# Moving all elementwise work from GpSimd to VectorE in a hybrid S5 + latent-attention layer, with a three-operation recurrence

## The chip, the cores and the metric

One core of a Trainium2 chip runs the whole program. The metric is device time in microseconds. Before the change the median of 3 runs is 2492.51 us (2489.13 to 2495.65).

## What is computed

One layer is applied to a prompt (512 tokens) and to a sample group (8 sequences of 8 tokens over a paged cache of 1024 positions), with the same weights. Cut to what matters here:

```
proj = x @ w_in                    # split: u (1024) | cq (512) | ckv (512) | kr (64)
bu   = einsum('bsgh,gph->bsgp', u, b_bar)          # S5: 64 groups, 64 complex states
h    = associative_scan(a_bar, bu)                 # h[t] = a_bar*h[t-1] + bu[t]
y    = real(einsum('bsgp,ghp->bsgh', h, c)) + d*u ; g = gelu(y)
out  = g * sigmoid(g @ w_glu + b_glu)
q    = (rms_norm(cq) @ w_uq) ; ckv = rms_norm(ckv) ; krope = rope(kr)
o    = softmax(q_lat.ckv + q_rope.krope) @ ckv     # prompt causal, sample over pages
x    = layer_norm(alpha*x + concat(out, o@w_uv) @ w_out)
x    = layer_norm(alpha*x + (silu(x@w_gate) * (x@w_up)) @ w_down)
```

All is float32. A product of two float32 matrices is made of three matmuls on rounded parts (`hi` by ScalarE, `lo = value - hi`).

## The kernel before, in words

The 576 token columns are held in two halves of 288. Stages follow each other in time: the input product (17 blocks of 128 output columns, each 96 matmuls 128x288) with S5's parameters, chunk sums, recurrence and taps beside it (0 to about 305 us of the profile); queries and prompt attention with S5's output (to about 500); sample attention, gate and output product with the first layer norm (to about 960); the feed-forward part (to the end), whose last 200 us hold the sums of w_down and the second layer norm.

A planner (`Clock`) records every instruction at build time: it keeps an estimated end time for each engine and tile, and generator fibers (`merge`, `drive`) are resumed when their data is estimated to be ready, so PE's order is written out by these estimates. A scheduler then orders each engine's queue by priority. All instructions are issued through one helper line, so every row of the profile says L180 and is told apart by the names of its tiles. Each engine runs its queue in order; SP's queue issues most DMAs.

Where the change acts:

- `sooner` chose between VectorE (DVE) and GpSimd (POOL) for an elementwise instruction, by the planner's estimates. It serves `split` (the `lo` parts: tiles `wlo`, `xl`, `cktlo`, `cknlo`), `rope`, and the sums and layer norms of the output and feed-forward stages (tiles `z`, `g`, `m`, `xl`, `Ah`, `Al`, `QS`, `T`, which are buffers used again under old names).
- `s5_states` makes for each of 8 chunks of 8 channel groups the factor `G` (four products, two sums, a transpose to `Gt`) and then PE's sums `Gt * U` into `S`. Two products (`Gx`, `Gy`) were on POOL. `U` is the chunk of u, written to DRAM (`us`) and read back in another order.
- `s5_scan` runs 63 steps over blocks of 8 tokens. Tile `S` was stored state first, block last (so one block's 64 numbers lie 72 apart), with five DVE instructions a step. At its end `S` went to DRAM (`Sd`) in four DMAs; `s5_out` reads it as `H2` (tile `H` in the rows).
- `s5_taps` makes for each chunk `P` (from `pw` and `bc`) and `BB`, all on POOL, and PE multiplies them (tile `ks`).
- `weights` builds the ring of later weights; its first two are of w_kv, used right after the queries of heads 0 and 1.

Of the kernel before, what the change touches and what calls it, by code (L numbers as in the profile page):

```python
# [7 lines left out]
F32 = mybir.dt.float32  # L8
# [154 lines left out]
class Clock:  # L163
# [356 lines left out]
class Layer:  # L520
# [248 lines left out]

    def place(self, j):  # L770

        j -= 16
        if j < 2:
            return None
        if j == 2:
            hi, lo = self.ff.tile([128, 1024], F32R, name="E"), self.cst.tile([128, 1024], F32R, name="rp")
            return [[x[:, 256 * i:256 * i + 256] for x in (hi, lo)] for i in range(4)]
        if j == 3:
            return [list(x) for x in zip(self.t4[:4], self.t4[4:])]
        a, b = (('T2', 'B22'), ('B11', 'B21'))[j // 2 - 2]  # L780
        k = j % 2 * 2
        return self.X[a][k:k + 2] + self.X[b][k:k + 2]

# [187 lines left out]
    def s5_side(self, done, lat):  # L971
        yield from self.s5_params(done)
        yield lambda: done['u']
        self.s5a = lat.enter_context(self.pool("s5a"))

        def states():
            with self.pool("s5b") as self.s5b:
                yield from self.s5_states(done)
            done['s5'] = True
            yield from self.s5_scan()  # L980
# [75 lines left out]
    def s5_params(self, done):  # L1056
# [5 lines left out]
        with self.pool("s5t") as tp:  # L1062
# [113 lines left out]
            nc.vector.tensor_copy(self.a8, V[:, 8])  # L1176

            Q = new((128, 10, 2, 128))
            for g2 in range(2):
                p = self.mmp(bufs=4)  # L1180
                for pb in range(2):
                    for i, e in enumerate((1, 2, 4, 9)):
                        nc.tensor.matmul(p[:, pb, 64 * i:64 * i + 64], sel[:, 2 * g2 + pb],
                                         V[:, e].rearrange("p r k -> p (r k)"), start=True, stop=True)
                yield
                for i in range(4):
                    nc.scalar.activation(Q[:, i].rearrange("p r (k a b) -> p b r k a", a=2, b=2)[:, :, :, :, g2],
                                         p[:, :, 64 * i:64 * i + 64].rearrange("p b (r k) -> p b r k", r=2), AF.Copy)
                yield
# [44 lines left out]

    def s5_states(self, done):
# [3 lines left out]
        pt = nc.gpsimd.tensor_tensor  # L1239
        self.S = self.s5a.tile([128, 32, 2, NC], F32, name="S")  # L1240
        self.h0s = self.s5a.tile([128, 32, 2, 8], F32, name="h0s")
        nc.sync.dma_start(self.h0s, io['h0s'].rearrange("p (a b c) -> p a b c", a=32, b=2))

        def load(ck):
            bq = p.tile([128, 2, 16, 16], F32, name="bq", bufs=2)
            nc.sync.dma_start(bq, io['s5bq'][ck].rearrange("p (r a b) -> p r a b", r=2, a=16))
            return bq

        bq = load(0)
        prev = None  # L1250
        for ck in range(9):
            cur = None
            if ck < 8:
                yield lambda: done['u'] > ck
                yield self.when(self.us[ck])
                U = self.load_U(p, ck)
                nb = load(ck + 1) if ck < 7 else None
# [9 lines left out]
                yield self.when(x, y)  # L1267
# [4 lines left out]
                cur = (U, Gt, ck)  # L1272
                bq = nb
            if prev:
                U, Gt, pk = prev
                yield self.when(U, Gt)
                ps = self.mmp(bufs=4)
                for g in range(8):
                    for r in range(2):
                        o = (g // 2 % 2) * 2 * NC + r * NC  # L1280
                        nc.tensor.matmul(ps[64 * (g % 2):64 * (g % 2) + 64, g // 4, o:o + NC],
                                         Gt[:, r, g], U[:, g], start=True, stop=True)
                yield
                nc.scalar.activation(self.S[:, 4 * pk:4 * pk + 4].rearrange("p (a k) r c -> p a (k r c)", a=2),
                                     ps[:, :, :HALF], AF.Copy)
            prev = cur

    def s5_scan(self):
        nc, io, S = self.nc, self.io, self.S
        tt, pt = nc.vector.tensor_tensor, nc.gpsimd.tensor_tensor  # L1290
        w = self.s5a.tile([128, 32, 2, 8], F32, name="scw")
        b8 = lambda r: self.a8[:, r, :, None].to_broadcast([128, 32, 8])
        h = self.h0s
        for (r, ra, op) in ((0, 0, OP.add), (0, 1, OP.subtract), (1, 0, OP.add), (1, 1, OP.add)):
            tt(w[:, :, r], h[:, :, r if ra == 0 else 1 - r], b8(ra), OP.mult)
            tt(S[:, :, r, PC:], S[:, :, r, PC:], w[:, :, r], op)
        so2 = self.s5a.tile([128, 32, 2, 8], F32, name="scw")
        nc.vector.tensor_copy(so2, S[:, :, :, PC:])
        nc.sync.dma_start(io['o_ss'].rearrange("p (k r b) -> p k r b", r=2, b=8), so2)
        yield self.lag('DVE')  # L1300
        ab = self.a8[:, 0, :, None].to_broadcast([128, 32, 2])
        t1 = self.s5a.tile([128, 32, 2], F32, name="sc1")
        t2 = self.s5a.tile([128, 32, 2], F32, name="sc2")
        nai = self.s5a.tile([128, 32], F32, name="nai")
        nc.vector.tensor_scalar(nai, self.a8[:, 1], -1.0, None, op0=OP.mult)
# [8 lines left out]
        nc.gpsimd.tensor_copy(so, S[:, :, :, PC - 1])  # L1314
        yield self.when(so)
        nc.sync.dma_start(io['o_sp'].rearrange("p (k r) -> p k r", r=2), so)
        for r in range(2):
            for g2 in range(2):
                nc.sync.dma_start(self.Sd[64 * r:64 * r + 64, g2::2, 1:PC], S[64 * g2:64 * g2 + 64, :, r, :PC - 1])

    def s5_taps(self):

        nc, io, pool = self.nc, self.io, self.s5k
        pt = nc.gpsimd.tensor_tensor
# [10 lines left out]
        def powers():  # L1335
            for ck in range(8):
# [14 lines left out]
                X = X.rearrange("p a b c -> p (a b c)")[:, :128].rearrange("p (g h) -> p g h", g=8)  # L1351
                pt(BB[:, :, :16], bc[:, 0], fb(0), OP.mult)
                pt(X, bc[:, 1], fb(1), OP.mult)
                pt(BB[:, :, :16], BB[:, :, :16], X, OP.add)
                for s in (slice(4), slice(4, 8)):
# [4 lines left out]
                    yield self.lag('POOL')  # L1360
# [1095 lines left out]
```

## Time and profile before

| | |
|---|---|
| median of 3 runs | 2492.51 us |
| profiled execution | 2493.54 us, of which the span is 2491.5 |
| PE busy | 2350.2 us (94%) |
| DVE busy | 1957.2 us (79%) |
| ACT busy | 1077.4 us (43%) |
| POOL busy | 444.4 us (18%) |

The span is the time from the first to the last instruction that the profiler recorded; 2 us lie around it. A busy PE can be slow: the column PEclk gives the share of the full TensorE clock that was granted. PE is the engine with the most work; where it idles, the row behind the idle time names the instruction that released it. POOL works up to about 950 us and after 2300 us; between 960 and 2000 us it has nothing to do.

### The profile page before, as it was taken

The numbers are of one execution on the slowest core, as the hardware profiler recorded it, in microseconds if no ns is written. First come the engines' busy times: TensorE is split into PE (matmuls) and PEld (weight loads), VectorE is DVE, ScalarE is ACT, GpSimd is POOL, SyncE is SP. The second block draws the span as 40 slices with busy tenths as digits, with TensorE's granted clock in tenths as the row PEclk, the third lists the DMA queues.
The fourth block names the chain that finished last, engine by engine and source line by source line (L and its number), as shares of the span: only waits on it lengthen the run. The fifth ranks groups of instructions, "written<-read, shape, count | busy, mean of one in ns | idle before, by whom it ended". The sixth has DMA issues, their size and how long they took to land.

```text
span 2491.5 us, 45005 instructions
## 1 busy us (share of the span) xinstructions
PE 2350.2 (94%) x17220; PEld 2297.1 (92%) x17220; DVE 1957.2 (79%) x3313; ACT 1077.4 (43%) x1685; POOL 444.4 (18%) x390
## 2 busy tenths in 40 slices
PE   8988989999899989999999999999999999979995
PEld 7877989998898989999999999999999999979994
DVE  7759766778778886999988878887778876755978
ACT  4221355656555544433333333333336644553133
POOL 2682010143344550000000000000000000000335
PEclk9988999999999989999999999999999999989997
DMA  6563456478765556455433333333236765677622
GB/s 216 178 183 120 105 161 199 144 240 294 243 194 165 198 172 217 174 183 190 164 113 132 120 113 132 112 123 107 107 113 208 254 186 143 170 205 251 243 94 76
DMA packets 219161, 419.90 MB, mean 169 GB/s; under 512 B 62210, under 2 KB 127106, under 8 KB 217154
## 3 DMA queue, kind: packets, MB, share of 16 engines
q1 hardware_dynamic: 187154, 359.66, 43.5%
q10 hardware_dynamic: 30064, 44.98, 5.0%
q0 software_dynamic: 1728, 12.39, 2.8%
q8 instruction: 135, 2.21, 0.4%
q14 instruction: 80, 0.66, 0.1%
HBM read 337.52 MB, written 83.64 MB: 169 GB/s over the span
## 4 chain that ended last, share of the span: by engine, by line
PE 56%; DVE 12%; DMA 11%; issue 3%; ACT 3%; POOL 1%; SPq 0%; ACTq 0%; DVEq 0%; POOLq 0%
PE mm L180 34%; PE sc L180 21%; DVE wlo L180 3%; DVE z L180 2%; DVE xl L180 2%; DMA wraw<-w_gu 2%; DMA hraw<-hd 1%; PE po L180 1%; DMA cktraw<-ckt 1%; DMA mraw<-so 1%; DVE T L180 1%; ACT whi L180 1%; DMA T<-pa 1%; DVE Al L180 1%; DVE g L180 1%
## 5 line engine op out<-in xcount | busy, mean ns | idle before, releaser
L180 PE MATMUL mm<-xh,whi 128*128 128x288 f32 x2272 | 606.1, 305 | 17.5 <-ACT xh L180 9.6
L180 PE MATMUL mm<-xh,wlo 128*128 128x288 f32 x2272 | 607.1, 304 | 13.6 <-DVE wlo L180 13.3
L180 PE MATMUL mm<-xl,whi 128*128 128x288 f32 x2272 | 605.7, 303 | 4.5 <-DVE xl L180 4.0
L180 PEld LDWEIGHTS mm<-xh,whi 128*128 128x128 f32 x2272 | 409.8, 193 | 26.8 <-ACT xh L180 10.9
L180 PEld LDWEIGHTS mm<-xh,wlo 128*128 128x128 f32 x2272 | 410.6, 193 | 20.9 <-DVE wlo L180 18.0
L180 PEld LDWEIGHTS mm<-xl,whi 128*128 128x128 f32 x2272 | 411.1, 193 | 7.8 <-DVE xl L180 5.0
L180 PE MATMUL sc<-z,whi 128*128 128x288 f32 x1470 | 350.8, 297 | 1.2 <-ACT z L180 0.6
L180 ACT ACTIVATE whi<-wraw 128x1024 fp32r<-128x1024 f32 (+2 forms) x159 | 173.8, 1094 | 281.1 <-PE mm L180 187.2
L180 DVE TENSOR_TENSOR wlo<-wraw,whi 128x1024 fp32r<-128x1024 f32 (+2 forms) x150 | 214.4, 1431 | 89.7 <-ACT whi L180 87.4
L180 ACT ACTIVATE whi<-E 128x1024 fp32r<-128x1024 f32 x120 | 127.2, 1060 | 334.7 <-issue 193.1
L180 PEld LDWEIGHTS sc<-z,whi 128*128 128x128 f32 x1470 | 250.7, 189 | 2.3 <-ACT whi L180 1.0
L180 ACT ACTIVATE whi<-rp 128x1024 fp32r<-128x1024 f32 x120 | 127.4, 1061 | 256.9 <-issue 191.3
L180 DVE TENSOR_TENSOR wlo<-E,whi 128x1024 fp32r<-128x1024 f32 x120 | 146.7, 1223 | 94.0 <-ACT whi L180 93.5
L180 POOL DMA_DIRECT2D pa<-m x6 | 5.3, 890 | 1200.2 <-ACT m L180 1200.2
L180 PE MATMUL mm<-T,H 128*128 128x288 f32 x1200 | 217.3, 296 | 1.8 <-ACT T L180 1.7
L180 DVE TENSOR_TENSOR wlo<-rp,whi 128x1024 fp32r<-128x1024 f32 x120 | 146.5, 1221 | 72.1 <-ACT whi L180 71.9
L180 PEld LDWEIGHTS mm<-T,H 128*128 128x128 f32 x1200 | 180.8, 189 | 2.5 <-ACT T L180 2.2
L180 PE MATMUL mm<-Ah,wlo 128*128 128x288 f32 x480 | 137.5, 308 | 14.6 <-DVE wlo L180 12.7
L180 PE MATMUL sc<-Ah,H 128*128 128x288 f32 x552 | 144.3, 297 | 6.6 <-DVE H L180 3.2
L180 PE MATMUL mm<-Ah,H 128*128 128x288 f32 x552 | 144.4, 297 | 4.2 <-ACT Ah L180 4.2
L180 PE MATMUL sc<-z,wlo 128*128 128x288 f32 x490 | 145.8, 298 | 0.9 <-DVE wlo L180 0.9
L180 PE MATMUL sc<-g,whi 128*128 128x288 f32 x490 | 144.8, 295 | 0.9 <-ACT g L180 0.8
(505 smaller groups left out, 5493.6 us busy)
## 6 DMA issues: line engine op xcount, KB each, us to landing
wraw<-w_gu SPq DMA_DIRECT2D x145, 512.0 KB, 3.2
qns<-w_gu SPq DMA_DIRECT2D x59, 512.0 KB, 3.3
wraw<-w_out SPq DMA_DIRECT2D x56, 512.0 KB, 3.9
wraw<-w_dq SPq DMA_DIRECT2D x43, 512.0 KB, 3.4
cktraw<-ckt SPq DMA_DIRECT2D x64, 320.0 KB, 4.5
cknraw<-ckn SPq DMA_DIRECT2D x64, 256.0 KB, 3.9
hd<-QS ACTq DMA_DIRECT2D x16, 1008.0 KB, 4.1
wraw<-w_in SPq DMA_DIRECT2D x14, 1024.0 KB, 5.8
```

The lines of the kernel that those rows point to most:

```text
L180: r = f(*a, **k)
```

## The change

Six edits: `sooner` always returns VectorE; the products of `s5_states` and `s5_taps` that were on GpSimd go to VectorE; `S` is stored block first, so that one recurrence step is one product of 128 numbers and two sums of 64; `G` is made by a fiber of its own, up to one chunk ahead of PE's sums, and `B`'s first load and the state `h0` stand earlier; `S` is copied by ScalarE into a staging tile (`hst`, two buffers, four pieces of eight state groups) and goes to `Sd` in 16 DMAs; the first two weights of the later ring are split at an earlier priority. GpSimd keeps memsets, small casts and the DMAs that add.

```diff
     def sooner(self, op, out, *ins):
-        t = self.ready(*ins)
-        d, p = (max(t + 150, self.end[e]) + self.cost(e, op, out, ins) for e in ('DVE', 'POOL'))
-        return self.gpsimd if p + 500 < d else self.vector
+        return self.vector
...
         self.ring = Ring(self, self.wst, "w", 1024, items, ahead=100)
+        at = self.tc.cur_priority
+        self.tc.cur_priority = max(at - 400, 0)
+        self.ring.split(1)
+        self.tc.cur_priority = at
...
-        yield from self.merge((states(), 3), (taps(), 1))
+        yield from self.merge((states(), 1e9), (taps(), 1))
...
-        self.S = self.s5a.tile([128, 32, 2, NC], F32, name="S")
+        self.S = self.s5a.tile([128, NC, 2, 32], F32, name="S")
...
-                pt(x, B[1], E[1], OP.mult)
-                pt(y, B[1], E[0], OP.mult)
+                yield self.when(bq)
                 tt(G[:, 0], B[0], E[0], OP.mult)
+                tt(x, B[1], E[1], OP.mult)
                 tt(G[:, 1], B[0], E[1], OP.mult)
+                tt(y, B[1], E[0], OP.mult)
...
+                yield ('t', nc.ready(U, made[ck]) + 4000)
                 ps = self.mmp(bufs=4)
...
+                for a in range(2):
+                    k = 4 * ck + 2 * a
+                    nc.scalar.activation(self.S[:, :, :, k:k + 2].rearrange("p c r k -> p k r c"),
+                                         ps[:, a, :HALF].rearrange("p (k r c) -> p k r c", k=2, r=2), AF.Copy)
...
         for c in range(1, PC):
-            tt(t1, S[:, :, :, c - 1], ab, OP.mult)
-            tt(t2[:, :, 0], S[:, :, 1, c - 1], nai, OP.mult)
-            tt(t2[:, :, 1], S[:, :, 0, c - 1], self.a8[:, 1], OP.mult)
-            tt(S[:, :, :, c], S[:, :, :, c], t1, OP.add)
-            tt(S[:, :, :, c], S[:, :, :, c], t2, OP.add)
-            yield self.lag('DVE', 2000)
+            tt(x, S[:, c - 1, :, None, :].to_broadcast([128, 2, 2, 32]), A, OP.mult)
+            tt(S[:, c], S[:, c], x[:, 0], OP.add)
+            tt(S[:, c], S[:, c], x[:, 1], OP.add)
+            yield self.lag('DVE', 1500)
...
-        for r in range(2):
-            for g2 in range(2):
-                nc.sync.dma_start(self.Sd[64 * r:64 * r + 64, g2::2, 1:PC], S[64 * g2:64 * g2 + 64, :, r, :PC - 1])
+        n = 32 // 4
+        for k in range(0, 32, n):
+            yield ('t', hp.avail("hst", 2))
+            st = hp.tile([128, n, 2, PC - 1], F32, name="hst", bufs=2)
+            nc.scalar.activation(st, S[:, :PC - 1, :, k:k + n].rearrange("p c r k -> p k r c"), AF.Copy)
+            yield self.when(st)
+            for r in range(2):
+                for g2 in range(2):
+                    nc.sync.dma_start(self.Sd[64 * r:64 * r + 64, 2 * k + g2:2 * (k + n):2, 1:PC],
+                                      st[64 * g2:64 * g2 + 64, :, r])
...
-        pt = nc.gpsimd.tensor_tensor
+        pt = nc.vector.tensor_tensor
...
-                    yield self.lag('POOL')
+                    yield self.lag('DVE', 2500)
```

VectorE's queue where the first two chunks of S5 are worked on. Before (`wlo` is the low part of a w_in block, waited for by that block's matmuls):

```order
L180 TENSOR_TENSOR wlo<-wraw,whi 128x2048
L180 TENSOR_SCALAR nai<-a_276 128x32
L180 TENSOR_TENSOR scw<-h0s,a_276 128x32x8 x2
L180 TENSOR_TENSOR G<-bq,eq 128x512 x2
L180 TENSOR_TENSOR G<-G,Gx 128x512
L180 TENSOR_TENSOR G<-G,Gy 128x512
L180 STREAM_TRANSPOSE Gt<-G 128x1024
L180 TENSOR_TENSOR G<-bq,eq 128x512 x2
```

The same place of the changed kernel:

```order
L180 TENSOR_TENSOR P<-bc,pw 128x576
L180 TENSOR_TENSOR G<-G,Gx 128x512
L180 TENSOR_TENSOR P<-bc,pw 128x576
L180 TENSOR_TENSOR PX<-bc,cf 128x128
L180 TENSOR_TENSOR BB<-bc,cf 128x8x16
L180 TENSOR_TENSOR G<-G,Gy 128x512
L180 TENSOR_TENSOR wlo<-wraw,whi 128x2048
L180 TENSOR_TENSOR Gx<-bq,eq 128x512
```

The products of the taps (`P`, `PX`, `BB`) and `Gx`, `Gy` now stand between VectorE's own, and a `wlo` stands behind a `P` that waits for the DMAs of `pw` and `bc`.

SP's queue at the end of the recurrence, before:

```order
L180 DMA Sd<-S 2048x1x63 x3
L180 DMA o_sp<-so 128x64
L180 DMA Sd<-S 2048x1x63
L180 DMA wraw<-w_kv 128x1024 x2
L180 DMA U<-us_60 128x576
```

And in the changed kernel:

```order
L180 DMA Sd<-hst 64x8x63 x2
L180 DMA o_sp<-so 128x64
L180 DMA Sd<-hst 64x8x63 x13
L180 DMA wraw<-w_kv 128x1024 x2
L180 DMA Sd<-hst 64x8x63
L180 DMA U<-us_60 128x576
```

The loads of w_kv stand behind 15 of the 16 pieces of the state, the last of which come from the fourth staging copy.

## Rows read from the trace of the kernel before

**Rows 1.** Busy time by stage: each line is a stretch (us), its length, then busy us (and instruction count) of PE, PEld, DVE, ACT and POOL, then the granted share of TensorE's clock, the DMA share and GB/s.

```profile
0.00:320.00 320.00, 276.37 (x2179) 267.57 (x2180) 241.39 (x578) 98.29 (x133) 137.54 (x145) 0.93 0.53 161
320.00:500.00 180.00, 176.16 (x1262) 166.97 (x1261) 126.69 (x301) 108.67 (x226) 13.81 (x36) 0.98 0.54 165
500.00:960.00 460.00, 426.10 (x2908) 405.88 (x2906) 372.85 (x540) 252.97 (x395) 201.35 (x143) 0.94 0.66 216
960.00:2000.00 1040.00, 1033.63 (x7739) 1028.95 (x7739) 864.05 (x1358) 420.36 (x595) 0.00 (x0) 1.00 0.43 150
2000.00:2300.00 300.00, 282.55 (x2021) 275.86 (x2020) 188.63 (x295) 144.29 (x237) 11.12 (x13) 0.96 0.66 185
2300.00:2491.50 191.50, 155.36 (x1121) 151.92 (x1120) 163.64 (x245) 52.83 (x102) 80.63 (x55) 0.92 0.40 144
```

**Rows 2.** PE in order of time: start, length, what, and in brackets PE's idle time before it and what ended it.

```profile
39.67 0.85 PE L180 MATMUL mm<-xl,whi 128*128 128x288 f32 x2 [4.02 <-DVE xl L180]
...
127.50 0.66 PE L180 MATMUL mm<-P,BB 128*32 128x128 f32 x8 [5.12 <-POOL P L180]
143.91 0.43 PE L180 MATMUL mm<-P,BB 128*32 128x128 f32 x8 [2.33 <-POOL P L180]
...
210.40 0.85 PE L180 MATMUL mm<-xh,wlo 128*128 128x288 f32 x2 [5.93 <-DVE wlo L180]
239.63 0.64 PE L180 MATMUL mm<-ones,rssq 128*96 128x1 f32 x3 [5.19 <-DVE rssq L180]
318.08 0.38 PE L180 MATMUL mm<-whi,xh 128*128 128x256 f32 x1 [4.66 <-ACT whi L180]
639.86 0.80 PE L180 MATMUL po<-cknlo,PT 128*128 128x512 f32 x1 [3.45 <-DVE cknlo L180]
904.94 0.40 PE L180 MATMUL mm<-Ah,wlo 128*128 128x288 f32 x1 [2.73 <-DVE wlo L180]
920.06 0.61 PE L180 MATMUL mm<-Ah,wlo 128*128 128x288 f32 x1 [6.93 <-DVE wlo L180]
2453.08 0.40 PE L180 MATMUL mm<-g,Ah 128*128 128x288 f32 x1 [2.91 <-DVE Al L180]
```

**Rows 3.** DVE and POOL in order of time, in three places; columns as in rows 2.

```profile
15.24 7.97 DVE L180 SCALAR_TENSOR_TENSOR sp<-sp,sp 128x32 f32<-128x32 f32 x6
28.37 0.52 DVE L180 SCALAR_TENSOR_TENSOR sp<-sp,sp 128x32 f32<-128x32 f32 x4
15.16 1.32 POOL L180 TENSOR_TENSOR wlo<-wraw,whi 128x512 fp32r<-128x512 f32 x1 [13.98 <-ACT whi L180]
16.44 1.43 POOL L180 TENSOR_TENSOR xl<-xr,xh 128x576 fp32r<-128x576 f32 x1
...
917.58 2.42 DVE L180 TENSOR_TENSOR wlo<-wraw,whi 128x1024 fp32r<-128x1024 f32 x1
923.47 1.21 DVE L180 TENSOR_TENSOR wlo<-wraw,whi 128x1024 fp32r<-128x1024 f32 x1
...
2475.08 5.65 POOL L180 TENSOR_TENSOR Al<-Al,xh 128x576 f32<-128x576 f32 x3
2479.39 1.95 DVE L180 TENSOR_TENSOR z<-z,xh 128x576 f32<-128x576 f32 x1
2481.93 0.74 DVE L180 TENSOR_TENSOR z<-z,xh 128x576 f32<-128x576 f32 x1
```

**Rows 4.** Groups of DVE and ACT instructions by shape up to 350 us: busy us, mean ns of one, idle time before them.

```profile
L180 DVE TENSOR_TENSOR G<-bq,eq 128x512 f32<-128x512 f32 x16 | 19.7, 1269 | 0.2
L180 DVE TENSOR_TENSOR G<-G,Gy 128x512 f32<-128x512 f32 x8 | 10.9, 1368 | 1.0 <-POOL Gy L180 1.0
L180 DVE TENSOR_TENSOR wlo<-wraw,whi 128x512 fp32r<-128x512 f32 x9 | 6.1, 688 | 6.0 <-ACT whi L180 6.0
L180 DVE TENSOR_TENSOR sp<-sp 128x128 f32<-128x128 f32 x7 | 1.8, 286 | 0.1
L180 ACT ACTIVATE whi<-wraw 128x1024 fp32r<-128x1024 f32 x5 | 5.2, 1054 | 2.5 <-DMA wraw<-w_uq 2.5
```

**Rows 5.** Groups of POOL instructions by shape up to 350 us, in the same columns.

```profile
L180 POOL TENSOR_TENSOR P<-P,PX 128x576 f32<-128x576 f32 x16 | 29.8, 1862 | 0.9
L180 POOL TENSOR_TENSOR PX<-bc,pw 128x576 f32<-128x576 f32 x16 | 21.0, 1314 | 0.7
L180 POOL TENSOR_TENSOR P<-bc,pw 128x576 f32<-128x576 f32 x16 | 20.0, 1270 | 23.2 <-DMA pw<-pwd 23.2
L180 POOL TENSOR_TENSOR PX<-bc,cf 128x128 f32<-128x128 f32 x8 | 4.6, 569 | 8.8 <-DMA bc<-s5bc 8.8
```

**Rows 6.** DVE in one step of the recurrence that POOL does not disturb; columns as in rows 2.

```profile
212.36 0.59 DVE L180 TENSOR_TENSOR S<-S,sc 128x64 f32<-128x64 f32 x2
212.98 0.27 DVE L180 TENSOR_TENSOR sc<-S,a 128x64 f32<-128x64 f32 x1
213.17 0.20 DVE L180 TENSOR_TENSOR sc<-S,nai 128x32 f32<-128x32 f32 x1
213.28 0.19 DVE L180 TENSOR_TENSOR sc<-S,a 128x32 f32<-128x32 f32 x1
213.40 0.58 DVE L180 TENSOR_TENSOR S<-S,sc 128x64 f32<-128x64 f32 x2
```

More of the change, by code (lines that the diff above doesn't have):

```diff
@@ L979, in states @@
             done['s5'] = True
-            yield from self.s5_scan()
+            yield from self.s5_scan(done, lat)
         def taps():
@@ L1238, in s5_states, with factors @@
         tt = nc.vector.tensor_tensor
-        pt = nc.gpsimd.tensor_tensor
-        self.S = self.s5a.tile([128, 32, 2, NC], F32, name="S")
[L1241 to L1257, printed above, removed]
+        self.S = self.s5a.tile([128, NC, 2, 32], F32, name="S")
+        bq = self.bq[0]
+        made, used = {}, [0]
+        def factors(bq):
+            for ck in range(8):
+                yield lambda: used[0] >= ck - 1
+                nb = self.load_B(ck + 1) if ck < 7 else None
                 G = p.tile([128, 2, 16, 2, 16], F32, name="G")
@@ L1271, in s5_states, with sums @@
                 nc.vector.transpose(Gt.rearrange("p r g n -> p (r g n)"), G.rearrange("p r a b c -> p (r a b c)"))
-                cur = (U, Gt, ck)
+                made[ck] = Gt
                 bq = nb
-            if prev:
-                U, Gt, pk = prev
-                yield self.when(U, Gt)
+                yield self.lag('DVE', 1500)
+        def sums():
+            for ck in range(8):
+                yield lambda: done['u'] > ck
+                yield self.when(self.us[ck])
+                U = self.load_U(p, ck)
+                yield lambda: ck in made
+                yield ('t', nc.ready(U, made[ck]) + 4000)
                 ps = self.mmp(bufs=4)
@@ L1281, in s5_states @@
                         nc.tensor.matmul(ps[64 * (g % 2):64 * (g % 2) + 64, g // 4, o:o + NC],
-                                         Gt[:, r, g], U[:, g], start=True, stop=True)
+                                         made[ck][:, r, g], U[:, g], start=True, stop=True)
+                used[0] = ck + 1
                 yield
-                nc.scalar.activation(self.S[:, 4 * pk:4 * pk + 4].rearrange("p (a k) r c -> p a (k r c)", a=2),
-                                     ps[:, :, :HALF], AF.Copy)
@@ L1286, in s5_states, with s5_scan @@
-            prev = cur
-    def s5_scan(self):
+                for a in range(2):
+                    k = 4 * ck + 2 * a
+                    nc.scalar.activation(self.S[:, :, :, k:k + 2].rearrange("p c r k -> p k r c"),
+                                         ps[:, a, :HALF].rearrange("p (k r c) -> p k r c", k=2, r=2), AF.Copy)
+        yield from self.merge((sums(), 1e9), (factors(bq), 1e9))
+    def s5_scan(self, done, lat):
         nc, io, S = self.nc, self.io, self.S
-        tt, pt = nc.vector.tensor_tensor, nc.gpsimd.tensor_tensor
-        w = self.s5a.tile([128, 32, 2, 8], F32, name="scw")
+        tt = nc.vector.tensor_tensor
+        w = self.s5l.tile([128, 32, 2, 8], F32, name="bq", bufs=2)
@@ L1299, in s5_scan @@
+        so2 = self.s5l.tile([128, 32, 2, 8], F32, name="bq", bufs=2)
+        nc.scalar.activation(so2, new, AF.Copy)
         nc.sync.dma_start(io['o_ss'].rearrange("p (k r b) -> p k r b", r=2, b=8), so2)
         yield self.lag('DVE')
[L1301 to L1305, printed above, removed]
@@ L1315, in s5_scan @@
         yield self.when(so)
         nc.sync.dma_start(io['o_sp'].rearrange("p (k r) -> p k r", r=2), so)
-        for r in range(2):
-            for g2 in range(2):
-                nc.sync.dma_start(self.Sd[64 * r:64 * r + 64, g2::2, 1:PC], S[64 * g2:64 * g2 + 64, :, r, :PC - 1])
+        yield lambda: 'taps' in done
+        hp = lat.enter_context(self.pool("s5h"))
+        n = 32 // 4
[5 more added lines that the diff above has]
+            for r in range(2):
+                for g2 in range(2):
+                    nc.sync.dma_start(self.Sd[64 * r:64 * r + 64, 2 * k + g2:2 * (k + n):2, 1:PC],
+                                      st[64 * g2:64 * g2 + 64, :, r])
```

41 lines of the change are left out of this document (26 added, 15 removed).

## The prediction, made before the changed kernel was run

> **What bounds the kernel now.** I read the stage table first [rows 1]. From 960 to 2000 us PE is busy 1033.63 of 1040 us at the full clock: the change has nothing to take there, and POOL does nothing there either. What can be won lies in three stretches. From 0 to 320 us PE idles 43.6 us, and the granted clock is 0.93, that is some 22 us more lost at the lower of its two levels (1.2 against 2.4 GHz): 66 us. From 500 to 960 it is 33.9 us of idle time and a clock of 0.94 (28 us): 62 us. After 2300 it is 36 us of idle time, nearly all behind the last dense products, where VectorE works almost alone. In just these three stretches POOL is busy: 137.5, 201.4 and 80.6 us. From 2000 to 2300 PE also loses time, but POOL has 11 us there, the DMAs that add, which stay.
>
> PE's waits come next [rows 2]. In the first stretch the long ones end with POOL's `P` (5.12 and 2.33), a `wlo` (5.93), the sums of squares (5.19), the first `xl` (4.02) and w_kv's high part on ACT (4.66). At 904.94 and 920.06 PE waits 2.73 and 6.93 for a `wlo`.
>
> Then why VectorE is late [rows 3]. At 15.24 six instructions on 32 numbers take 7.97 us, 1.3 each, as long as one POOL instruction (1.32, 1.43); at 28.37, with POOL idle, four of the same take 0.52. The `wlo` at 917.58 takes 2.42, at 923.47 it takes 1.21. The `z` at 2479.39 takes 1.95, the one at 2481.93, when POOL has ended, 0.74. So an instruction of VectorE that meets POOL is held up, and POOL is itself slower: three of 128x576 take 5.65 us. I went through all VectorE rows with the undisturbed duration of their shape (0.69 for 128x512 [rows 4], 0.75 for 128x576 and 1.21 for 128x1024 [rows 3], about 0.45 for 128x288). 212 of them took over 0.1 us more, the first at 15.24, the last at 2479.39 [rows 3], and 211 of these overlap a POOL instruction. The excess is 55 us up to 350 us, 63 us from 500 to 960 and 43 us after 2280: 161 us.
>
> **The change part by part.** *Load of VectorE.* 308 POOL instructions move (110, 143 and 55 in the three stretches). At VectorE's undisturbed durations the first lot is 57 of 128x576 at 0.75 (43 us), 20 of 128x512 at 0.69 (14), 24 of 128x128 at 0.29 (7) and 9 small ones (2): 66 us [rows 3 to 5]. The other two lots, at 0.42 to 0.75 by shape, come to some 72 and 34 us. VectorE takes 172 us and gets 161 back: +11 in the first stretch, +9 in the second, -9 in the third. A pair shows the exchange: one POOL and one VectorE instruction of 128x576 together now take 1.9 us, on VectorE alone 2 x 0.75 = 1.5.
>
> *Recurrence.* A step takes 1.04 us (212.36 to 213.40) [rows 6]. Two dependent sums take 0.62 of it, so 0.31 each; independent ones are 0.19 and 0.11 apart. The new step is a product of 128 numbers and two sums, each on the result before. Bounds: 3 x 0.19 = 0.57 and 0.31 x 3 = 0.93; I take 0.85, near the upper, since all three depend on each other. 63 steps give back 63 x 0.19 = 12 us (7 to 30). So the first stretch ends near zero: some 241 us of VectorE work beside 276 us of PE.
>
> *Waits of PE, first stretch.* The waits on `P` and, since the tap products now stand later in PE's order than the chunk sums, the 2.33 behind it, the `wlo` at 210.40 (it stood behind a recurrence slowed by POOL) and the sums of squares at 239.63 make 18.6 us. I let four fifths go: 15 us. Such a wait is followed by a stretch at the lower clock, and the 22 us lost to it belong to some eight waits; with half of these gone I take 12 us. The wait at 39.67 stays: the parameter instructions before that `xl` are fewer microseconds, but three more `xl` and `wlo` are queued before it.
>
> *What the change adds.* `P` now waits on VectorE's queue for the DMAs of `pw` and `bc`, for which POOL had waited 23.2 and 8.8 us [rows 5]; behind it stand the next `wlo` and so the next block of PE. The first is the long one, when the parameters have just been written, and VectorE has a block's lead then; 0 to 10 us on the path, I take 1. The hand-over of the state is dearer. Four staging copies of 1008 numbers cost ACT 4 x 1.05 = 4.2 us (row of 1024 numbers [rows 4]); the third waits for the landing of the first's four DMAs, and ACT's copies for the keys and queries stand behind it; the loads of w_kv stand behind 15 of the 16 DMAs on SP. The wait for w_kv's high part, 4.66 at 318.08 [rows 2], is where that ends. Earlier priority for its split can't help while its load stands there. Bounds: -5 (the wait goes) and +12; I take +6, clock included.
>
> First stretch: -15 - 12 + 1 + 6 = -20 us. Bounds -50 (all but the start) and +12 (the additions alone).
>
> *500 to 960.* The waits on VectorE's and POOL's low parts and sums add up to some 23 of the 33.9 us; 904.94 and 920.06 alone make 9.7, and the `wlo` there stands behind VectorE rows at half pace. I let 9 us go, and 6 of the 28 lost to the clock: -15. Bounds: -42 (all 23, and two thirds of the clock), +9 (no wait shorter, VectorE's 9 us more on the path).
>
> *After 2300.* VectorE is the chain behind the last dense products, about 2443 to 2486. From 2425 its excess by the rows is some 21 us, and 19 instructions of 128x576 at 0.75 (14 us) come over: -7 on the path. The waits before 2440 are mostly for loads of the partial sums: -1. Together -8, bounds -14 and +5.
>
> The ring's order, the copies on ACT of `S` in blocks, and the earlier loads cost nothing: ACT is busy 98 of 320 us [rows 1], and the loads stand where the queue waits anyway. If ACT's cover went, 16 more copies at some 0.4 us would cost 6 us.
>
> Sum, against the profiled execution (2493.54): -20 - 15 - 8 = -43, so 2450.5. The median of the runs is 1 us lower, so the forecast is **2449 us**.
>
> A page speaks for keeping POOL: the Trainium skill, "Perfetto Trace Analysis", section "Optimizing Scalar/DVE Operations", says that with VectorE saturated, offloading to ScalarE or even GpSimd may make sense, and adds that between these two it might not help because they share a port. The row at 2479.39 beside 2481.93 is the second half of that sentence; the first half would be the rival on the slower side, below.
>
> **The rivals.** *The planner becomes right (2412).* Its estimates know nothing of the hold-up; between 960 and 2000, where POOL is idle, its order leaves PE 6 us of 1040. If the other two stages come near that, two thirds of the 66 + 62 us less the fixed start and the loads go: some -70, with -11 at the end. For it: 211 of 212 rows. Against it: waits for DMAs in the sample stage (216 GB/s over it) that no engine sets.
>
> *VectorE's queue as the bound of the first stage (2479).* 241 us of work in order beside PE's 254 (276 less the 22 of the clock), with waits for `pw`, `bc` and the norms in it: each wait of VectorE is then one of PE. The first stage gives 0, the second -7, the end -7: -14. For it: `P` in front of a `wlo`. Against: VectorE idled 78 us of the 320, and by my sum of row durations along both queues each `wlo` still ends some 5 us before its block.
>
> *Slower (2535): VectorE is full and nothing comes back.* Were the long VectorE rows long for another reason than POOL, the 172 us would be added whole. Where VectorE is already the chain, after 2300, that is +34; from 500 to 960 the 72 us fill the 87 us of its idle time, and I put +8 on the path: +42. It decides if `z` of 128x576 in the last 20 us still takes 1.9 us. Against it: rows 3, three times.
>
> *Nothing changes in time (2491):* the waits go and the loads that stand behind them are met instead, in both stages, with -2 left from the end. For it: the chain of waits in the sample stage has loads in it; against it, the first stage has few.
>
> The Trainium skill, "SBUF — State Buffer", section "SBUF: two separate sides", calls the shared port an exclusive lock, held for a whole instruction, under which the other engine fully blocks. By that rule POOL's 414 us of moved work could have cost VectorE up to that much, and the sum for VectorE's load would be 172 - 414 = -242; the rows give 161 of excess, and many VectorE instructions that overlap POOL took no longer than usual. I keep the rows; the rule would favour the first rival.
>
> **How the numbers follow.** Forecast 0.47 (own range 2428 to 2470), planner right 0.18, VectorE's queue 0.21, slower 0.09, nothing 0.05. Three runs of this kernel lie within 0.13% of their median; less than 0.3% (7.5 us) counts as no change. The forecast, the first rival and all but a little of the second are faster: 0.47 + 0.18 + 0.20 = 0.85. No change: 0.05 + 0.01 = 0.06. Slower: 0.09. The range reaches from just below the first rival to above the second, 2404 to 2487; it leaves out the slower case, half of the unchanged one and the low tail.
>
> **What would show it.** Right: POOL below 30 us; VectorE busy within 20 us of 1957; `G` products at 0.69 against 1.27; the recurrence near 0.85 a step; no 128x576 row of VectorE above 1 us; the gap before the taps' matmuls and the `wlo` of 920 gone; the first product with w_kv about 20 us earlier than 318, with a longer wait in front of it. Wrong: a `wlo` behind a `P` that waits for a DMA, PE idle in the first 320 us above 40 us, or a last chain after PE as long as now (48 us).

## The result and the profile after

The changed kernel takes 2433.25 us (median of 4 runs, 2427.78 to 2434.27) against 2491.36 for the kernel before: a ratio of 0.9756 (95% interval 0.974 to 0.9772), 58 us less. The forecast was 2449, its own range 2428 to 2470, the whole range 2404 to 2487. The profiled execution has a span of 2425.9 us, at the lower end of its runs, so differences between the two profiles come to 65.6 us and not to 58. One run below, e12, was profiled in an execution that something disturbed from end to end (4971.7 us): its trace is not read, and its ratio leaves that execution out.

Busy time by stage, in the columns of [rows 1]:

```profile
0.00:320.00 320.00, 297.89 (x2426) 288.66 (x2427) 247.71 (x618) 133.86 (x192) 13.14 (x42) 0.97 0.58 181
320.00:500.00 180.00, 175.95 (x1307) 168.66 (x1306) 132.98 (x315) 107.66 (x212) 21.05 (x36) 1.00 0.60 188
500.00:960.00 460.00, 434.01 (x3006) 413.69 (x3005) 373.96 (x642) 255.24 (x402) 4.19 (x4) 0.97 0.66 216
960.00:2000.00 1040.00, 1035.11 (x7754) 1030.45 (x7752) 870.17 (x1372) 425.69 (x609) 1.91 (x2) 1.00 0.43 149
2000.00:2300.00 300.00, 279.30 (x1990) 272.97 (x1989) 199.21 (x312) 126.47 (x204) 8.63 (x10) 0.95 0.68 205
2300.00:2426.00 126.00, 101.28 (x748) 100.24 (x746) 96.40 (x211) 48.01 (x101) 0.00 (x0) 0.90 0.28 97
```

A stretch of the clock on the wall holds more work after than before (PE's count in the first line is 2426 against 2179), so the stages are compared by marks in the work: the start of the 6th and 10th block of 96 dense products of the input projection, the end of its 17 blocks (the start of an 18th, which is the first of the queries), the first product with w_kv, the first scores of the sample stage, the first product of the feed-forward (`sc<-z,whi`), the last of that name (`last dense`; PE still has other products behind it), and the end. In us, from the timelines of PE:

```
                      6th   10th   18th   w_kv  sample    ffn  last dense     end
before               87.3  175.9  303.7  318.1   498.1  997.3      2428.3  2491.5
after                78.0  149.7  260.3  280.9   462.0  943.0      2371.3  2425.9
difference           -9.3  -26.2  -43.4  -37.2   -36.1  -54.3       -57.0   -65.6
```

So 43.4 us are won before the 18th block, 6.2 of them given back at w_kv, 1.1 lost up to the sample stage, 18.2 won in it (481.0 against 499.2 us), 2.7 in the feed-forward, 8.6 behind the last dense product (54.6 against 63.2).

PE up to the 6th block and from there to the 18th, in the columns of [rows 1], before:

```profile
0.00:87.30 87.30, 75.48 (x520) 73.80 (x521) 56.49 (x158) 35.72 (x58) 23.05 (x27) 0.96 0.63 208
87.30:303.70 216.40, 189.82 (x1587) 183.27 (x1586) 170.01 (x401) 48.70 (x56) 104.64 (x101) 0.91 0.47 140
```

and after:

```profile
0.00:78.00 78.00, 72.03 (x521) 70.89 (x522) 48.20 (x170) 35.85 (x58) 0.99 (x10) 1.00 0.70 232
78.00:260.30 182.30, 177.77 (x1587) 172.30 (x1586) 158.70 (x368) 57.94 (x70) 1.23 (x6) 0.99 0.48 151
```

The matmuls are the same in number. Of the 43.4 us, 27.9 are PE's idle time (38.4 before, 10.5 after) and 15.5 its busy time, at a granted clock of 1.00 and 0.99 where it was 0.96 and 0.91.

PE's waits over 2 us up to 320 us, without the one of 5.4 us at the start that both kernels have, and after 2300, which answer to [rows 2]:

```profile
146.71 2.06 PE L180 MATMUL mm<-U,Gt 128*64 128x72 f32 x30 [3.71 <-DVE Gt L180]
280.89 0.58 PE L180 MATMUL mm<-whi,xh 128*128 128x256 f32 x1 [10.86 <-ACT whi L180]
2401.89 2.08 PE L180 MATMUL sc<-ones,xl 128*96 128x1 f32 x12 [4.62 <-DVE xl L180]
```

The waits for the first `xl`, for POOL's `P`, for the `wlo` at 210 and for the sums of squares are gone; the one in front of w_kv has grown from 4.66 to 10.86. One more is gone that [rows 2] does not show, for the load of `U`; in the kernel before it was:

```profile
169.22 0.47 PE L180 MATMUL mm<-U,Gt 128*64 128x72 f32 x3 [5.51 <-DMA U<-us]
```

VectorE in the start and in the last 20 us (columns as in [rows 3]), and its groups up to 350 us (as [rows 4]):

```profile
24.90 0.87 DVE L180 SCALAR_TENSOR_TENSOR sp<-sp,sp 128x32 f32<-128x32 f32 x7
2406.86 1.42 DVE L180 TENSOR_TENSOR z<-z,xh 128x576 f32<-128x576 f32 x2
2408.20 0.75 DVE L180 TENSOR_TENSOR g<-g,xh 128x576 f32<-128x576 f32 x1
```

```profile
L180 DVE TENSOR_TENSOR G<-bq,eq 128x512 f32<-128x512 f32 x16 | 10.3, 681 | 0.0
L180 DVE TENSOR_TENSOR G<-G,Gy 128x512 f32<-128x512 f32 x8 | 5.4, 681 | 0.0
L180 DVE TENSOR_TENSOR P<-P,PX 128x576 f32<-128x576 f32 x16 | 11.9, 745 | 0.0
```

Seven instructions of 128x32 take 0.87 us where six took 7.97; a `G` product takes 0.68 against 1.27, a `z` 0.75 against 1.95. I went through all VectorE rows again with the undisturbed duration of their shape: 162 us of excess before (as in the prediction, 161), 4 us after. GpSimd still has 16 sums with two inputs, those of the gates (`g<-xh,xl`): the "all" of the title and the list of what GpSimd keeps leave them out. Most of VectorE's few long rows after are beside them.

Two steps of the recurrence after, beside [rows 6]:

```profile
213.71 0.29 DVE L180 TENSOR_TENSOR h0s<-S,h0s 128x128 f32<-128x128 f32 x1
214.03 0.48 DVE L180 TENSOR_TENSOR S<-S,h0s 128x64 f32<-128x64 f32 x2
214.55 0.29 DVE L180 TENSOR_TENSOR h0s<-S,h0s 128x128 f32<-128x128 f32 x1
```

A step takes 0.84 us (213.71 to 214.55) against 1.04.

### The profile page after: what moved, and what is told of

Read it like the earlier page. It is cut to its first block, busy times and chain, and to the rows that moved or that the text cites. A ratio compares the mean times of both kernels' runs of the same rounds, so it can differ in the third digit from the quotient of the medians.

```text
span 2425.9 us, 44757 instructions
## 1 busy us (share of the span) xinstructions
PE 2323.5 (96%) x17220; PEld 2274.7 (94%) x17220; DVE 1920.4 (79%) x3465; ACT 1096.9 (45%) x1718; POOL 48.9 (2%) x93
## 4 chain that ended last, share of the span: by engine, by line
PE 70%; DMA 11%; DVE 11%; ACT 4%; issue 3%; SPq 1%; ACTq 0%; DVEq 0%
PE mm L180 46%; PE sc L180 23%; DVE wlo L180 2%; DMA cktraw<-ckt 2%; DMA wraw<-w_out 2%; DMA wraw<-w_gu 1%; ACT whi L180 1%; PE po L180 1%; DMA mraw<-hd 1%; DVE z L180 1%; DVE xl L180 1%; DMA wraw<-w_dn 1%; SPq L180 1%; DVE Al L180 1%; DMA hd<-m 1%
## 5 line engine op out<-in xcount | busy, mean ns | idle before, releaser
L180 PEld LDWEIGHTS mm<-xh,wlo 128*128 128x128 f32 x2272 | 406.3, 191 | 11.4 <-DVE wlo L180 8.2
L180 DVE TENSOR_TENSOR wlo<-wraw,whi 128x1024 fp32r<-128x1024 f32 (+2 forms) x159 | 201.3, 1267 | 67.8 <-ACT whi L180 66.8
L180 PE MATMUL sc<-g,wlo 128*128 128x288 f32 x490 | 144.4, 295 | 0.0
L180 PE MATMUL mm<-Ah,whi 128*128 128x288 f32 x480 | 133.7, 300 | 5.1 <-ACT whi L180 2.7
```

The costliest lines, as they stand in the source:

```text
L180: r = f(*a, **k)
```

## The experiments

Theory 1 is the prediction's: an instruction of POOL holds up VectorE's, and PE waits for VectorE. Theory 2: S5's new layout and shorter step bring the time. Theory 3: what cost the time were POOL's own late results. Times are medians of runs beside the kernel before on the same chip; that kernel's median lay between 2493.6 and 2497.3 in these runs. Differences between medians can be off by these few us; a difference of ratios, times 2494, is the safer figure. The marks of the kernels that follow:

```
                      6th   10th   18th   w_kv  sample    ffn  last dense     end
e1 chooser back      91.2  168.5  280.9  304.6   487.8 1000.0      2430.5  2493.3
e2 chooser gone      78.1  161.0  297.3  311.8   495.5  980.0      2406.3  2460.0
e3 S5 on GpSimd      79.3  158.5  286.6  303.0   486.2  978.9      2409.2  2463.1
e4 five instr.       79.3  149.9  261.6  282.9   458.3  947.0      2376.8  2430.5
e5 idle products     79.4  161.1  272.5  293.4   480.5  965.2      2394.2  2447.9
e6 idle memsets      77.9  149.8  261.5  282.3   467.7  952.2      2376.5  2430.2
e9 idle copies       79.0  153.1  264.3  285.4   471.8  950.7      2379.3  2433.0
```

**The two edits apart.** First the changed kernel with the old choice:

```diff
     def sooner(self, op, out, *ins):
-        return self.vector
+        t = self.ready(*ins)
+        d, p = (max(t + 150, self.end[e]) + self.cost(e, op, out, ins) for e in ('DVE', 'POOL'))
+        return self.gpsimd if p + 500 < d else self.vector
```

> The changed kernel with the old choice between VectorE and GpSimd for the sums and low parts; S5's own products stay on VectorE. Some 160 two-input instructions go back to POOL, nearly all from 500 to 960 us and in the last 120. Theory 1 (an instruction of POOL holds up VectorE's): VectorE's rows beside POOL are long again, the stretch from 500 to 960 is some 17 us longer, the end some 11, the start some 5 because POOL has low parts in the first 40 us: about 2433 + 33 = 2466. Theory 2 (the gain is S5's new layout and its shorter recurrence, whichever engine takes the rest): within 6 us of 2433.

Measured: 2493.22 us, ratio 0.9997 (0.9981 to 1.0014). All of the gain is gone, not the 33 us that theory 1 priced. Its PE in the first 50 us, and two of its waits up to 320 us (in all, times, longest):

```profile
0.00:50.00 50.00, 34.45 (x214) 33.41 (x215) 39.51 (x124) 21.23 (x32) 17.17 (x22) 0.90 0.72 252
```

```profile
PE mm L180 <- ACT whi L180: 15.2, 3, 13.9
PE mm L180 <- DVE xl L180: 8.2, 1, 8.2
```

PE does 214 products there, against 316 after. The 6th block starts 13 us later than after, the sample stage takes 512 us, the end 62.8. VectorE's excess is 13.7 us in the first 60, 66.6 from 480 to 960, 43.0 at the end: the stages in which GpSimd works again are the ones that are long. Theory 2 falls as the account of the whole gain: this kernel has the new layout and the three-instruction step.

The other way round, the same line alone in the kernel before:

```diff
-        t = self.ready(*ins)
-        d, p = (...)
-        return self.gpsimd if p + 500 < d else self.vector
+        return self.vector
```

> The kernel before with one edit: the choice between VectorE and GpSimd always gives VectorE; S5's products stay on GpSimd and the recurrence keeps its five instructions. Theory 1: the same three pieces are won as the first run loses, 17 + 11 + 5, so 2491 - 33 = 2458, with the first 320 us still holding waits of PE for POOL's P. Theory 2: 2485 to 2491. If the two edits are independent, this run's gain and the first run's loss are equal within 5 us.

Measured: 2461.78 us, ratio 0.9861 (0.9825 to 0.9897). The 32 us that were expected; but the same line is worth 60 in the changed kernel, so the edits are not independent. The marks say where: 9.2 us are won by the 6th block and 14.9 by the 10th, and only 6.4 are left at the 18th. With S5's products still on GpSimd, VectorE has 48 us of excess there, and a `wlo` (8.9 us at the longest) and the sums of squares (5.1) are met later in place of the start.

S5's products alone back on GpSimd, in the changed kernel:

```diff
-                tt(x, B[1], E[1], OP.mult)
+                nc.gpsimd.tensor_tensor(x, B[1], E[1], OP.mult)
...
-        pt = nc.vector.tensor_tensor
+        pt = nc.gpsimd.tensor_tensor
```

> The changed kernel with S5's products back on GpSimd (Gx and Gy, and the products for the taps); the new layout, the three-instruction step and factors made ahead stay. Theory 1: 96 instructions on POOL stretch VectorE's rows from 70 to 190 us by some 35 us together; PE waits for P and for a wlo behind the long rows, 10 to 20 us with the clock: 2443 to 2453. Theory 2: what counts is the new order and the step, so at most 4 us over 2433.

Measured: 2464.4 us, ratio 0.9877 (0.9845 to 0.9909), 31 us over the changed kernel and more than expected. The 18th block is 26 us later, VectorE's excess 45 us. Beside e2 it differs by the rewrite of S5 without its engine: 0.9877 against 0.9861, no gain that shows in the time. By the marks it is not nothing: e3 is 10.7 us ahead of e2 at the 18th block and 9.3 at the sample stage, which then takes it 8.2 longer (492.7 against 484.5), about what that stage differs among kernels with GpSimd nearly idle in it (below). So of the 43.4 us at the 18th block, in this order of edits and by one profile of each, the chooser makes 6.4, the rewrite of S5 with the smaller edits beside it (theory 2) 10.7, and taking S5's products off GpSimd 26.3.

**The recurrence.** Five instructions on the new layout:

```diff
-            tt(x, S[:, c - 1, :, None, :].to_broadcast([128, 2, 2, 32]), A, OP.mult)
+            tt(x[:, 0], S[:, c - 1, 0:1].to_broadcast([128, 2, 32]), A[:, 0], OP.mult)
+            tt(x[:, 1, 0], S[:, c - 1, 1], A[:, 1, 0], OP.mult)
+            tt(x[:, 1, 1], S[:, c - 1, 1], A[:, 1, 1], OP.mult)
```

> The changed kernel with a step of the recurrence in five instructions again, on the new layout: the product of 128 numbers in one of 64 and two of 32. A step goes from 0.85 to some 1.07 us, 63 steps 14 us. The scan's end sets when the state can be handed over, and behind that stand the loads of w_kv: theory 2, and the hand-over as the bound of the first stretch, give 8 to 14 us more: 2441 to 2447. If the scan has slack beside PE (100 us busy of 100 from 150 to 250), 2431 to 2437.

Measured: 2432.16 us, ratio 0.9753 (0.9722 to 0.9784): nothing. VectorE in one step:

```profile
213.73 0.43 DVE L180 TENSOR_TENSOR h0s<-S,h0s 128x64 f32<-128x64 f32 x3
214.08 0.47 DVE L180 TENSOR_TENSOR S<-S,h0s 128x64 f32<-128x64 f32 x2
214.59 0.43 DVE L180 TENSOR_TENSOR h0s<-S,h0s 128x64 f32<-128x64 f32 x3
```

The step did not grow: 0.86 us with five instructions, 0.84 with three. The three products overlap; what is shorter than before is the pair of sums, 0.47 against 0.59, on numbers that now lie side by side. So this run could not price a longer scan; it shows that the count of instructions was no price in this chain.

**The hold-up by itself.** 32 instructions on GpSimd whose result nobody reads; PE, VectorE and ACT issue what they issue in the changed kernel, in the same order:

```diff
                 done[0] = ck
+                for i in range(4):
+                    dum = pool.tile([128, 12, 2, 16], F32, name="dum")
+                    e0, e1 = [self.eq[:, r, 16 * ck:16 * ck + 12, :, None].to_broadcast([128, 12, 2, 16]) for r in range(2)]
+                    nc.gpsimd.eng.tensor_tensor(dum, e0, e1, OP.mult)
```

> The changed kernel, and beside it 32 products of 128x384 on GpSimd whose result nobody reads; PE, VectorE and ACT have their instructions in the same order as in the changed kernel. They start when eq is written, near 68 us, and last some 35 us. Theory 1 (an instruction of POOL with two inputs holds up VectorE's, whoever needs its result): the rows of 128x512 and 128x576 on VectorE between 68 and 105 us go from 0.68 to 1.0 or more, VectorE loses 10 to 20 us there, and the dense blocks behind come 5 to 15 us later: 2438 to 2448. Theory 3 (what cost the time before was that POOL's own results came late, not that it held VectorE up): no row of VectorE longer, 2430 to 2436.

Measured: 2449.84 us, ratio 0.9814 (0.9783 to 0.9846), 17 us over the changed kernel by the medians, 14 by the ratios. POOL's products by tile (L1401, since they do not go through the helper; shortest, median and longest in ns), VectorE in order of time, and its groups from 70 to 110 us:

```profile
L1401 POOL TENSOR_TENSOR dum<-eq x32: 830/1164/2766, 70.1 to 108.2; 128x384 f32<-128x384 f32 x32
```

```profile
76.17 1.32 DVE L180 TENSOR_TENSOR Gx<-bq,eq 128x512 f32<-128x512 f32 x1
77.41 1.32 DVE L180 TENSOR_TENSOR G<-bq,eq 128x512 f32<-128x512 f32 x1
78.65 1.32 DVE L180 TENSOR_TENSOR Gy<-bq,eq 128x512 f32<-128x512 f32 x1
```

```profile
L180 DVE TENSOR_TENSOR P<-P,PX 128x576 f32<-128x576 f32 x2 | 2.8, 1385 | 0.0
...
L180 DVE STREAM_TRANSPOSE Gt<-G 128x1024 f32<-128x1024 f32 x2 | 2.5, 1231 | 0.0
```

A 128x512 row goes from 0.68 to 1.32 us and `P` from 0.74 to 1.39, with nobody waiting for POOL. POOL's product takes 0.83 while VectorE is idle; of that, each VectorE row beside it pays 0.64. The two take turns: three rows of VectorE start 1.24 us apart. The transpose, with one input, stays at 1.23. One input alone does not spare an instruction, though: a pair of `TENSOR_SCALAR`, which read one array and constants, goes from 0.69 us in the changed kernel (first row) to 1.74 here (second row):

```profile
72.50 0.69 DVE L180 TENSOR_SCALAR sp<-sp,c 128x576 f32<-128x576 f32 x2 [3.90 <-ACT sp L180]
73.91 1.74 DVE L180 TENSOR_SCALAR sp<-sp,c 128x576 f32<-128x576 f32 x2 [3.90 <-ACT sp L180]
```

VectorE's excess is 15.6 us in 26 rows from 70 to 110 us, and the 10th block is 11.4 later, the 18th 12.2. This settles theory 1 against 3: the work on GpSimd costs although its results are not needed.

The same with other instructions, a memset and a copy in place of the product:

> As the run before, but the 32 instructions on GpSimd are memsets of 128x384, that have no input; they run from about 40 us on, beside VectorE's parameter instructions on 128x32. If any instruction of POOL holds VectorE up, these go from 0.19 us to some 0.5 and the parameters are 5 to 10 us later: 2436 to 2444. If only instructions that read do so, no row is longer, and the time is 2430 to 2436.

> As the run with 32 products that nobody reads, but each is a copy of 128x384: one input in place of two, POOL still beside VectorE's factors and tap products from about 70 us. If it is the second input that makes POOL hold up VectorE, the 128x512 rows stay at 0.68 us, and the dense blocks come within 2 us of the changed kernel: 2430 to 2437. If reading at all does it, the rows go to 1.0 or more and the blocks come 5 to 12 us later: 2438 to 2450.

Measured: memsets 2436.76 us, ratio 0.9774 (0.9747 to 0.9801), copies 2436.63, ratio 0.9762 (0.9746 to 0.9779); neither time tells them from the changed kernel; the marks are finer. The memsets ran from 40 to 54 us beside only a few VectorE instructions, none of them longer, and the 10th block starts 0.1 us later, the 18th 1.2: no hold-up seen, on little evidence. Of the copies, POOL's by tile and VectorE in order of time:

```profile
L1401 POOL COPY dum<-eq x32: 505/703/1092, 69.0 to 118.1; 128x384 f32<-128x384 f32 x32
```

```profile
74.32 0.68 DVE L180 TENSOR_TENSOR G<-bq,eq 128x512 f32<-128x512 f32 x1
74.92 0.99 DVE L180 TENSOR_TENSOR Gx<-bq,eq 128x512 f32<-128x512 f32 x1
75.83 0.99 DVE L180 TENSOR_TENSOR G<-bq,eq 128x512 f32<-128x512 f32 x1
```

A copy holds VectorE up too, by 0.31 us of its 0.51: 0.99 in place of 0.68. Over the 32 that is an excess of some 6 us, and blocks 3 to 4 us later. The first of the two answers falls: it is not the second input that does it. The second comes close for the rows (0.99, where it said 1.0 or more), and its price was too high.

**The wait in front of w_kv.** ACT's staging copies after are dearer than I took them (1.05 us), and the loads of w_kv stand behind the state's DMAs on SP:

```profile
L180 ACT ACTIVATE hst<-S x4: 1979/2040/2063, 253.9 to 269.3; 128x1008 f32<-128x1008 f32 x4
```

The DMAs on GpSimd's queue (`nc.gpsimd.dma_start` for `Sd`), and then also the copies turned (`nc.scalar.activation(st.rearrange("p k r c -> p c r k"), S[:, :PC - 1, :, k:k + n], AF.Copy)`):

> The changed kernel with the 16 DMAs that write the state (Sd) on GpSimd's queue in place of SP's, so that the loads of w_kv stand behind none of them. If SP's queue is what makes the first product with w_kv late, it comes 8 to 10 us earlier than 280.6 and the wait of 10.86 us in front of it goes: about 2424. If ACT is (its staging copies of 2.0 us each, and the rotary copies in front of whi), 0 to 4 us earlier: 2429 to 2434.

> The run before, with the four staging copies of the state in the order of the source: they read in rows of 8 numbers and write with the stride, where they read with a stride of 64 numbers. If it is the strided read that makes them 2.0 us, they come to 1.05 to 1.3, ACT gets 3 to 4 us back in front of whi, and the first product with w_kv is 2 to 4 us earlier than in the run before. If a stride costs the same on either side, they stay at 2.0 and nothing moves.

Measured: 2435.58, ratio 0.9771 (0.9738 to 0.9804), and 2433.74, ratio 0.9759 (0.9733 to 0.9785). In the first, the load of w_kv goes out 14 us earlier and the wait is as long; ACT's row, before `whi` at 281.33, is the four rotary copies:

```profile
259.65 1.14 SPq L180 DMA_DIRECT2D wraw<-w_kv  x2
```

```profile
PE mm L180 <- ACT whi L180: 11.6, 2, 11.3
```

```profile
278.53 2.78 ACT L180 ACTIVATE qrh<-qr 64x576 fp32r<-64x576 f32 x4
281.33 2.00 ACT L180 ACTIVATE whi<-wraw 128x1024 fp32r<-128x1024 f32 x2
```

So SP's queue alone was not what made it late, and neither answer came out: the product comes at 282.4, 1.5 us later. The queue was not out of play either. In the changed kernel ACT was done with the rotary copies at 278.8 and then waited for the load:

```profile
279.78 1.06 ACT L180 ACTIVATE whi<-wraw 128x1024 fp32r<-128x1024 f32 x1 [0.97 <-DMA wraw<-w_kv]
```

So there both ended within 1 us of each other. In e7, whose order on ACT is not the same, the fourth staging copy stands later (275.6 against 269.3), and ACT alone sets the end. The turned copies take 2.14 us (median) against 2.03: the stride costs on either side, and nothing moves, as the second answer said. Then the third and fourth copy off ACT, to GpSimd or to VectorE, with the DMAs still on GpSimd's queue:

```diff
-            nc.scalar.activation(st, S[:, :PC - 1, :, k:k + n].rearrange("p c r k -> p k r c"), AF.Copy)
+            if k < 2 * n:
+                nc.scalar.activation(st, ..., AF.Copy)
+            else:
+                nc.gpsimd.tensor_copy(st, ...)
```

> The changed kernel with the DMAs of the state on GpSimd's queue and the third and fourth staging copy on GpSimd too, so that ACT has neither in front of whi for w_kv. After the two runs that moved the DMAs and turned the copies, ACT's order is what is left as the cause of the wait of 10.86 us: the first product with w_kv comes 4 to 6 us earlier than 280.6, about 275 to 277, and the time is 2426 to 2431. If the chain from the last product of the norms over VectorE and ACT (rotary and its copies) is as long without the copies, it stays at 279 to 282.

> As the run before, with the third and fourth staging copy on VectorE. Here whi for w_kv stands in front of the four rotary copies on ACT, another 2.8 us earlier; VectorE gets two copies between its own steps of that chain. If ACT's order is the cause, the first product with w_kv comes 6 to 10 us earlier than 280.6 and the time is 2423 to 2429; if VectorE's two copies push its own chain back, 2430 or more.

Measured: 2436.87, ratio 0.9758 (0.9741 to 0.9774), and 2441.5, ratio 0.9774 (0.9757 to 0.9792). The first product with w_kv comes at 278.6 and 275.2, against 282.4 in e7, which has its DMAs on the same queue, and 280.9 in the changed kernel. So ACT's order makes 3.9 and 7.3 us of the 11.3 that PE waits in e7; against the changed kernel it is 2.3 and 5.7, less than both expectations. The time doesn't follow: it is over both of the ranges that went with them. PE's waits of the second from 255 to 320 us:

```profile
PE sc L180 <- ACT kh L180: 4.3, 1, 4.3
PE mm L180 <- DVE qnl L180: 3.8, 1, 3.8
PE mm L180 <- DVE wlo L180: 2.3, 1, 2.3
```

The one long wait has become three short ones, and the sample stage is entered at 462.1 and 467.6 (462.0 after) and takes 493 and 491 us. None of these four beats the changed kernel.

**The sample stage alone.** The old choice, held to 480 to 960 us of the plan:

```diff
-        return self.vector
+        t = self.ready(*ins)
+        if not 480e3 < self.end['PE'] < 960e3:
+            return self.vector
+        d, p = (...)
+        return self.gpsimd if p + 500 < d else self.vector
```

> The changed kernel with the old choice between VectorE and GpSimd in the sample stage alone (480 to 960 us of the plan); the start and the end are as in the changed kernel. If GpSimd's work there is what the stage lost, VectorE has 50 to 65 us of excess again in it, the stage from the first scores of the sample part to the first product of the feed-forward (481 us in the changed kernel, 499 in the one before, 512 with the choice back everywhere) goes to 495 to 512, and the time to 2447 to 2464. If the 18 to 31 us came from the stage being entered at another point of the plan, it stays at 481 to 490 and the time within 7 us of 2433.

Measured: 2445.41 us, ratio 0.9791 (0.9774 to 0.9807). It has no marks. By the ratios, 0.9791 - 0.9756, it is 9 us over the changed kernel, by the medians 12: between the two answers, under the 14 that theory 1 asked for. So GpSimd's work in that stage costs some 9 to 12 us. The rest of the 18 that lie between the two profiles is how a stage falls out from one order or execution to the next: e6 issues the same as the changed kernel there, and its stage takes 484.5, that of e3 492.7, with GpSimd nearly idle in both. Over the eleven profiles with GpSimd nearly idle there the stage takes 478.8 (e9) to 492.8 us (e10), and over the four whose PE, VectorE and ACT issue the same, 478.8 to 484.6.

## Why the prediction was right, and where it wasn't

**The mechanism was right.** That VectorE's long rows are POOL's doing stands on e5, where only POOL's work was added. The ledger closed as forecast: 161 us of excess, 4 left. What the excess is worth in time was sized too small where PE waits behind it, in the first stretch.

**The first stretch was too small: -20 forecast, -37.2 measured.** The step that failed is "The wait at 39.67 stays". It went: in e1 it comes back as 8.2 us, with 13.7 us of excess in VectorE's parameter instructions. I had counted three more instructions in the queue and not weighed that 11.3 of the 13.8 us of excess up to 60 us, in my own list of rows, lie in front of that `xl`. Up to the 6th block it is worth 9.3 us (5.8 of idle time, 3.5 of busy time), and it was forecast at nothing. The second step is the sum of the other waits: 15 less 1 for the new waits on DMAs were forecast, and between the 6th and the 18th block PE idles 22.0 us less (26.6 against 4.5). The four waits that I named make 18.6; the list did not have the 5.5 for the load of `U`, and no run shows why that one went. The clock was sized near: 12 forecast for the whole stretch, and the same matmuls keep PE busy 12.1 us less there and the 3.5 before.

**The hand-over was sized right for a partly wrong reason.** +6 forecast, 6.2 measured (43.4 to 37.2). But that "the loads of w_kv stand behind 15 of the 16 DMAs" is only half of it: without that the product came no earlier (e7). The copies that I took at 1.05 us take 2.0, and with two of them off ACT it came 3.9 us earlier than in e7, and 7.3 where `whi` also went in front of rotary copies (e10, e11). The wait is not one that pays when removed.

**The recurrence: the figure was right, the reason wrong.** 0.85 forecast, 0.84 measured. I derived it from three instructions in place of five; e4 has five at 0.86. My price for a dependent sum (0.31) belonged to the old layout; on the new one it is 0.26 (214.03 to 214.55 for two).

**The sample stage:** -15 forecast, 18.2 between the profiles, of which e12 assigns 9 to 12 to the change of engine. The rest is within what the stage differs from profile to profile, so that the forecast comes this near is in part luck. **The end:** -8 forecast, -8.6 measured; e2 and e3, with POOL idle there, have 53.7 and 53.9 us behind the last dense product, e1 62.8.

**Rivals.** The planner made right (2412) was not reached: the sample stage still has PE idle some 26 us by the table. VectorE's queue as the bound did not show: the waits for `Gt` and `P` add up to 4.5 us. The slower case falls with the `z` of 0.75 us. Two of the signs I named were missed: POOL is busy 48.9 us and not under 30, since the sums of the gates (18.3 us) and the issues of its DMAs (10.6) stay. 12 of these sums I had counted among the 308 instructions that move; 296 moved. And VectorE is busy 1920 us and not within 20 of 1957. I had priced each instruction that moves by its whole row, and rows that follow each other overlap (two `z` of 0.75 take 1.42 us together), which busy time counts once. How much of the 37 us that makes, no run takes apart.

I had weighed the Trainium skill, "SBUF — State Buffer", section "SBUF: two separate sides", as saying that POOL's 414 us could cost VectorE as much, and kept the rows. The page's lock binds VectorE's instructions that have two inputs from SBUF, against POOL's that read it, and those in a mode that uses both of VectorE's ports. e5, e6 and e9 agree with the first (two inputs held, transposes not; products and copies hold, memsets not seen to); that `TENSOR_SCALAR` was held too would fit the second, but no run shows its mode. The 414 us was my error: POOL's rows are long because they wait for VectorE too. In e5 products of 0.83 us show 1.14 on the mean, and the 32 of them, 36.4 us of rows, cost VectorE 15.6.

What stays open: why the sample stage of e1 takes 512 us where the kernel before, with as much excess there, takes 499.

## What to carry to other kernels

An engine off the critical path is not free if it slows one that is on it: look for rows of one shape with two durations, and for what runs beside the long ones, before crediting an offload. Price each wait with the lower clock behind it, and look at the first wait of a stage first, since what is won there is only kept if the later waits of the same chain go too (e2 kept 6 of its 15 us). A wait that is shown to have a cause need not be worth removing: with the copies gone from ACT, PE met the next three.

## What was not expected of the hardware

- Beside a POOL product of 128x384 a VectorE row of 128x512 takes 0.64 us more, beside a POOL copy 0.31; a transpose on VectorE was not held up at all (1.23 us), a pair of `TENSOR_SCALAR` by 1.05. In the kernel before, VectorE's instructions on 32 numbers took 1.3 us each beside POOL's and 0.13 without [rows 3]: the small ones lose most for their size.
- Three independent VectorE instructions on 64 or 32 numbers take 0.43 us together, one on 128 numbers 0.29: in a chain of dependent steps, more instructions cost next to nothing here, while two dependent sums went from 0.59 to 0.48 us by their layout alone.
- ACT's copy of 1008 numbers a partition takes 2.04 us when it turns the order as it reads and 2.14 as it writes, against 1.05 for 1024 in order.
